# A hybrid mLSTM and GLA layer step: 60 loads and small transfers move from SyncE's DMA queue to GpSimd's

## The chip, the cores and the metric

The kernel runs on one core of one Trainium2 chip. The metric is the device time of the program in microseconds (us).

## The reference

One layer, fp32, for 256 prompt positions of one sequence and one further position of 8 decode sequences: T = 264 columns in all, D = 2048.

```
p = x @ w_in                                # 13 column groups: mLSTM q/k, v, i, f, o, z; GLA q, k, v, gate, z; two merge gates
q, k = silu(causal conv of width 4 (qk))    # 4 heads of 256
h, C', n', m' = mlstm(q, k, v, i, f, C, n, m)     # decode: C' = dec * C + w k v^T;  h from q . C'
ya = headnorm(h) * sigmoid(o) * silu(z) @ w_pa
o, S' = gla(gq, gk, gv, log gate, S)              # decode: S' = exp(gate) * S + k v^T;  o = q . S'
yb = headnorm_rms(o) * silu(bz) @ w_pb
y = (sigmoid(g_a) * ya + sigmoid(g_b) * yb) @ w_out
out = layernorm(alpha * x + y) * ln_g + ln_b      # returned with all new states
```

What matters here are the decode states: C is 8 x 4 x 256 x 256 and S is 8 x 4 x 128 x 256, 8 MB and 4 MB, each read, updated and written once.

## The kernel before

**Weights.** All products with a weight are TensorE products with the weight block as the stationary side and 264 columns moving. The weights come as 262 pieces of 128 x (8 x 128) fp32, 512 KB each. `load_raw` (L181) loads a piece on SyncE into one of 4 buffers (raw); `cast_piece` splits it: ACT rounds it (hi, L203), DVE subtracts (lo, L204). For each of a piece's 8 row blocks there are three matmuls: hi by x's high part (L223), hi by its low part (L224), lo by the high part (L227).

**Side work.** Between the weight products, generators do the rest in small steps; `pump` takes some steps after each unit. Each step is recorded with a priority, and a scheduler puts the instructions of ACT, DVE, GpSimd and SyncE in an order of its own; TensorE's order is that of the program text. An engine, and a DMA queue, takes its instructions in that order: one that waits holds up those behind it. 20 slots of 4 KB per partition (`t4`) are shared by raw results, spread rows and state chunks; a load waits until its slot's former content has been used, or stored.

**The two decode generators.** `g_a_decode` first puts k and q rows into a small DRAM tile (kq_d, L512), reads n (L507), and works through C in 16 chunks of 512 KB: `load` (cch, L526), ACT scales (L555), DVE adds k v^T (L571) and takes the product with q (L573), and GpSimd stores (sC, L564). The k and q rows come from kq_d, spread over all 128 partitions by `spread_rows` (kb, qb, L489), 512 KB each, 8 times. `g_gla_rows` writes exp(gate), k and q rows to rows_d (L674). `g_gla_decode` works through S in 8 chunks: `load` (sch, L778), and for every second chunk three spread tiles ga, gk, gq (L489); for each half chunk ACT forms gkv (L805), DVE multiplies (L807), adds (L808), multiplies by gq (L809) and reduces (L810). GpSimd stores the chunk (sS, L813).

`g_b_norm` follows: ACT squares (L822), DVE adds the two halves into ns (L824), once for each of four heads, TensorE sums over partitions with a matrix of constants (L829), and ACT and DVE do the rest (L831 to L838). In `g_a_prompt` GpSimd stores pC (L476); in `g_gla_prompt` TensorE does L707 on gq and gk. `g_ln_rows` loads the rows of the final norm (lgf L947, lbb L952).

Before the change SyncE issues all loads, and the stores to the DRAM tiles; GpSimd issues the stores of states.

Of the kernel before, what the change touches and what calls it, by code (L numbers as in the profile page):

```python
# [83 lines left out]
def body(ctx, tc, xT, wbig, wsmall, par, cmask, lmask, sel, rowc, gate, wgu, cT, sT, nst, cst, lnr,  # L84
         y, yd, pC, pn, pm, pconv, pS, sC, sn, sm, sS):
    nc = tc.nc
    V, A, G, PE = nc.vector, nc.scalar, nc.gpsimd, nc.tensor
# [12 lines left out]
    def t4(shape, name, dt=F32):  # L100
        return b4.tile(shape, dt, tag="b4", name=name)
# [21 lines left out]
    def side_ps():  # L123
        return ps_s.tile([128, 512], F32, tag="sd", name="sd")
# [19 lines left out]
    def P(name, j=0, n=None):  # L144
        o, w = PAR[name]
        return par_sb[:, o + j:o + (w if n is None else j + n)]
# [6 lines left out]
    def f(ap):  # L153
        return ap.bitcast(F32)
# [331 lines left out]
    def spread_rows(dst, src):  # L486

        n = src.shape[0] * src.shape[1]
        nc.sync.dma_start(out=dst.rearrange("p b d -> p (b d)"),  # L489
                          in_=src.rearrange("r d -> (r d)").unsqueeze(0).to_broadcast([128, n]))  # L490

    def g_a_decode():
        qT, kT, dw, decb = st["qT"], st["kT"], st["dw"], st["decb"]
        num, dmx, avd = st["num"], st["dmx"], st["avd"]
        qkd = one.tile([128, 2, H, NB, 2], F32, tag="qkd", name="qkd")
        for x, src in enumerate((qT, kT)):
            for q in range(2):
                V.tensor_copy(out=qkd[:, x, 2 * q:2 * q + 2].rearrange("p h b t -> p h t b"),
                              in_=src.slot(q)[:, :, L:T].rearrange("p (h t) b -> p h t b", t=2))
        yield 0.5  # L500
        qr = tmp.tile([64, 128], F32, tag="t1", name="qr", bufs=T1_BUFS)
        kr = tmp.tile([64, 128], F32, tag="t1", name="kr", bufs=T1_BUFS)
        nr = tmp.tile([64, 128], F32, tag="t1", name="nr", bufs=T1_BUFS)
        pt = side_ps()
        for x in range(2):
            PE.transpose(out=pt[0:64, x * 128:x * 128 + 128], in_=qkd[:, x].rearrange("p h b t -> p (h b t)"), identity=ident)
        nc.sync.dma_start(out=nr, in_=nst)  # L507
        A.copy(out=qr, in_=pt[0:64, 0:128])
        V.tensor_scalar(out=kr, in0=pt[0:64, 128:256], scalar1=dw[:, 1:2], scalar2=None, op0=ALU.mult)
        kq_d = dram.tile([2, 64, 128], F32, name="kq_d")  # L510
        for x, src in enumerate((kr, qr)):
            nc.sync.dma_start(out=kq_d[x], in_=src)  # L512
        yield 0.5
        dn = one.tile([64, 1], F32, tag="dn", name="dn")
        dx = one.tile([64, H * NB], F32, tag="dx", name="dx")
        scr = tmp.tile([64, 128], F32, tag="t1", name="scr8", bufs=T1_BUFS)
        V.scalar_tensor_tensor(out=nr, in0=nr, scalar=dw[:, 0:1], in1=kr, op0=ALU.mult, op1=ALU.add)
        V.scalar_tensor_tensor(out=scr, in0=nr, scalar=1.0, in1=qr, op0=ALU.mult, op1=ALU.mult, accum_out=dn)
        V.tensor_scalar(out=dx, in0=rc_sb[:, NB:NB + H * NB], scalar1=dn, scalar2=None, op0=ALU.mult)
        G.dma_start(out=sn, in_=nr)  # L520
        chunks = {}

        def load(i):
            if i < 16:
                c = t4([128, 4, 256], "cch")
                nc.sync.dma_start(out=c, in_=cT[i])  # L526
                chunks[i] = c

        load(0)
        yield 0.6  # L530
        pb = side_ps()[:, 0:H * NB]
        PE.matmul(pb, lhsT=ones[0:64, :], rhs=dx, start=True, stop=True)
        pb = pb.rearrange("p (h b) -> p h b", b=NB)
        ad = tmp.tile([128, H, NB], F32, tag="t1", name="add", bufs=T1_BUFS)
        A.activation(out=ad, in_=pb, func=AF.Abs)
        V.tensor_tensor(out=dmx[:, :, L:T], in0=dmx[:, :, L:T], in1=ad, op=ALU.max)
        yield 0.4
        scr2 = tmp.tile([128, 256], F32, tag="t1", name="scr", bufs=T1_BUFS)
        steps = [(h, b0, e) for h in range(H) for b0 in (0, 4) for e in range(2)]
        rows = {}  # L540

        def spread(i):

            if i < 16:
                h, b0, _ = steps[i]
                rows[h, b0] = t4([128, 4, 256], "kb"), t4([128, 4, 256], "qb")
                for x in range(2):
                    spread_rows(rows[h, b0][x], kq_d[x, 16 * h + 2 * b0:16 * h + 2 * b0 + 8, :])

        def scale(i):  # L550
            h, b0, e = steps[i]
            load(i + 1)
            c = chunks[i]
            for b in range(4):
                A.activation(out=c[:, b, :], in_=c[:, b, :], func=AF.Copy, scale=decb[:, h, b0 + b:b0 + b + 1])  # L555

        spread(0)
        scale(0)
        yield 1.6
        for i, (h, b0, e) in enumerate(steps):  # L560
            if e == 0:
                spread(i + 2)
            if i:
                G.dma_start(out=sC[i - 1], in_=chunks.pop(i - 1))  # L564
            if i + 1 < 16:
                scale(i + 1)
            kb, qb = rows[h, b0]
            c = chunks[i]
            nd = num.t(2 * h + e)
            for b in range(4):  # L570
                V.scalar_tensor_tensor(out=c[:, b, :], in0=kb[:, b, :], scalar=avd[:, 2 * h + e, b0 + b:b0 + b + 1],  # L571
                                       in1=c[:, b, :], op0=ALU.mult, op1=ALU.add)
                V.scalar_tensor_tensor(out=scr2, in0=c[:, b, :], scalar=1.0, in1=qb[:, b, :], op0=ALU.mult,  # L573
                                       op1=ALU.mult, accum_out=nd[:, L + b0 + b:L + b0 + b + 1])
                if b % 2:
                    yield 2.1
        G.dma_start(out=sC[15], in_=chunks.pop(15))
        st["ad_done"] = True
# [83 lines left out]
    def g_gla_rows():  # L662
        gq, gk, la = st["gq"], st["gk"], st["la"]
        gd = one.tile([128, 3, H, NB], F32, tag="gd", name="gd")
        A.activation(out=gd[:, 0], in_=la[:, :, L:T], func=AF.Exp, scale=TAU_INV)
        V.tensor_copy(out=gd[:, 1], in_=gk[:, :, L:T])
        V.tensor_copy(out=gd[:, 2], in_=gq[:, :, L:T])
        yield 0.4
        pt = side_ps()
        PE.transpose(out=pt[0:96, 0:128], in_=gd.rearrange("p x h b -> p (x h b)"), identity=ident)  # L670
        rows = tmp.tile([96, 128], F32, tag="t1", name="rows", bufs=T1_BUFS)
        A.copy(out=rows, in_=pt[0:96, 0:128])
        rows_d = dram.tile([96, 128], F32, name="rows_d")
        nc.sync.dma_start(out=rows_d, in_=rows)  # L674
        st["rows"] = rows_d
        yield 0.3

# [93 lines left out]
    def g_gla_decode():  # L771
        rows, oT, bvd = st["rows"], st["oT"], st["bvd"]
        chunks = {}

        def load(i):
            if i < 8:
                c = t4([128, 4, 2, 128], "sch")
                nc.sync.dma_start(out=c, in_=sT[i])  # L778
                chunks[i] = c

        load(0)
        yield 0.1
        spread = {}

        def rows_of(h):
            if h < H:
                spread[h] = [t4([128, NB, 128], "g" + x) for x in "akq"]
                for i, x in enumerate(spread[h]):
                    spread_rows(x, rows[32 * i + 8 * h:32 * i + 8 * h + 8, :])
# [3 lines left out]
        for h in range(H):  # L793
            rows_of(h + 1)
            ab, kb, qb = spread.pop(h)
            for bh in range(2):
                load(2 * h + bh + 1)
                c = chunks.pop(2 * h + bh)
# [141 lines left out]
    def g_ln_rows():  # L940


        ln["G"], ln["B"] = [], []
        for hf in range(2):
            gf, hi = t4([128, 1024], "lgf"), t4([128, 1024], "lgh", F32R)
            gg = t4([128, 1024], "lgg", F32R)
            nc.sync.dma_start(out=gf, in_=lnr[:, hf * 1024:hf * 1024 + 1024])  # L947
            A.copy(out=hi, in_=gf)
            V.scalar_tensor_tensor(out=gg, in0=f(hi), scalar=P("lnm"), in1=gf, op0=ALU.mult, op1=ALU.add)
            ln["G"].append(gg)  # L950
            bb = t4([128, 1024], "lbb")
            nc.sync.dma_start(out=bb, in_=lnr[64:65, hf * 1024:hf * 1024 + 1024].to_broadcast([128, 1024]))  # L952
            ln["B"].append(bb)
            yield 2.0

# [131 lines left out]
    def drain():  # L1087
# [5 lines left out]
    waiting += [  # L1093
        (("gates_done", "avt_done"), g_a_prompt),
        (("gates_done", "avt_done"), g_a_decode),
        (("gq_done", "gk_done", "gates_done"), g_gla_rows),
        (("gq_done", "gk_done", "bvt_done", "rows", "ap_done"), g_gla_prompt),
# [213 lines left out]
```

## Time and profile before

| | |
|---|---|
| median of 3 runs | 845.92 us (845.65 to 849.77) |
| the profiled execution | 848.47 us, span 846.7 us |
| its granted TensorE clock, mean | 0.993 of full speed |
| DMA | 184.76 MB, mean 218 GB/s |

The profile is of one execution, taken by the hardware. Its span runs from the first to the last recorded instruction; 1.8 us of the execution's time lie around it. PE is TensorE, DVE VectorE, ACT ScalarE, POOL GpSimd, and SPq is SyncE's queue of DMA issues. L223 is line 223 of the kernel. An engine's idle time in front of an instruction is put down to what came last of all that it waited for.

### The profile page before, as it was taken

To read this page: it belongs to the slowest core of one execution; us is meant where nothing else is said; L and a number is where in the kernel's file an instruction comes from. 1 tells how busy PE (TensorE), PEld (TensorE's weight loads), DVE (VectorE), ACT (ScalarE), POOL (GpSimd) and SP (SyncE) were. 2 spreads that over 40 slices of the span, in tenths; PEclk is the share of its full clock that TensorE was granted. 3 is DMA by queue.
4 is the path that set the end of the run, shared out by engine and by line. 5 is a ranking of instruction groups with operands and counts; after the bars stand their busy time and mean duration, and the time that the engine had idled before them with its cause. 6 is when DMAs were issued, how large, how long until landed. Compare 5 with 4: busy or idle time off the path is not lost.

```text
span 846.7 us, 16717 instructions
## 1 busy us (share of the span) xinstructions
PE 826.7 (98%) x6773; PEld 813.3 (96%) x6773; DVE 591.4 (70%) x964; ACT 451.4 (53%) x706; POOL 45.1 (5%) x75
## 2 busy tenths in 40 slices
PE   6999999999999999999999998999999999999996
PEld 6999999999899999999999998999999999999995
DVE  6877668545658788757579979994445766666962
ACT  5655457545445653555467747764444444444633
POOL 0000000000001000001000000310000000000410
PEclk9999999999999999999999998999999999999998
DMA  8765565558586985678687799756555555576513
GB/s 318 246 203 181 159 188 171 165 163 262 214 284 225 381 292 189 198 262 312 203 300 243 231 335 329 240 171 203 184 178 184 185 177 177 185 248 214 176 49 103
DMA packets 54766, 184.76 MB, mean 218 GB/s; under 512 B 8209, under 2 KB 9153, under 8 KB 54689
## 3 DMA queue, kind: packets, MB, share of 16 engines
q1 hardware_dynamic: 50560, 169.28, 61.3%
q0 software_dynamic: 4128, 14.42, 4.3%
q8 instruction: 53, 0.87, 0.4%
q14 instruction: 25, 0.20, 0.1%
HBM read 166.98 MB, written 16.69 MB: 217 GB/s over the span
## 4 chain that ended last, share of the span: by engine, by line
PE 81%; DMA 7%; DVE 6%; ACT 2%; issue 2%; SPq 1%; ACTq 0%; POOLq 0%; POOL 0%; DVEq 0%
PE mm L223 25%; PE mm L224 25%; PE mm L227 24%; DMA raw<-wbig 4%; DMA cch<-cT 4%; DVE lo L204 2%; ACT hi L203 1%; DVE scr L573 1%; PE sd L707 1%; PE sd L464 1%; DVE cch L571 1%; ACT cch L555 1%; PE sd L754 0%; SPq L489 0%; PE sd L420 0%
## 5 line engine op out<-in xcount | busy, mean ns | idle before, releaser
L223 PE MATMUL mm<-xh,hi 128*128 128x264 f32 x1552 | 447.2, 289 | 10.2 <-ACT hi L203 9.8
L224 PE MATMUL mm<-xl,hi 128*128 128x264 f32 x1552 | 441.2, 285 | 0.0
L227 PE MATMUL mm<-xh,lo 128*128 128x264 f32 x1536 | 437.2, 285 | 0.5 <-DVE lo L204 0.5
L203 ACT CAST hi<-raw 128x1024 fp32r<-128x1024 f32 (+1 forms) x260 | 267.9, 1034 | 279.5 <-PE mm L224 245.1
L204 DVE TENSOR_TENSOR lo<-raw,hi 128x1024 fp32r<-128x1024 f32 (+1 forms) x260 | 314.9, 1214 | 144.2 <-ACT hi L203 142.0
L223 PEld LDWEIGHTS mm<-xh,hi 128*128 128x128 f32 x1552 | 294.0, 189 | 12.5 <-ACT hi L203 10.0
L224 PEld LDWEIGHTS mm<-xl,hi 128*128 128x128 f32 x1552 | 294.2, 190 | 0.3
L227 PEld LDWEIGHTS mm<-xh,lo 128*128 128x128 f32 x1536 | 290.1, 189 | 1.0 <-DVE lo L204 1.0
L223 PE MATMUL mm<-mh,hi 128*128 128x264 f32 x256 | 72.9, 285 | 0.0
L224 PE MATMUL mm<-ml,hi 128*128 128x264 f32 x256 | 72.7, 284 | 0.0
L227 PE MATMUL mm<-mh,lo 128*128 128x264 f32 x256 | 72.4, 283 | 0.0
L555 ACT ACTIVATE cch<-cch,decb 128x256 f32<-128x256 f32 x64 | 28.0, 500 | 38.6 <-DMA cch<-cT 38.6
L571 DVE SCALAR_TENSOR_TENSOR cch<-kb,avd,cch 128x256 f32<-128x256 f32 x64 | 29.0, 479 | 27.8 <-ACT cch L555 27.8
L227 PEld LDWEIGHTS mm<-mh,lo 128*128 128x128 f32 x256 | 48.2, 188 | 0.0
L223 PEld LDWEIGHTS mm<-mh,hi 128*128 128x128 f32 x256 | 48.1, 188 | 0.0
L224 PEld LDWEIGHTS mm<-ml,hi 128*128 128x128 f32 x256 | 48.1, 188 | 0.0
L224 PE MATMUL mm<-ybl,hi 128*128 128x264 f32 x128 | 36.4, 284 | 0.0
L227 PE MATMUL mm<-yah,lo 128*128 128x264 f32 x128 | 36.4, 284 | 0.0
L223 PE MATMUL mm<-ybh,hi 128*128 128x264 f32 x128 | 36.4, 284 | 0.0
L224 PE MATMUL mm<-yal,hi 128*128 128x264 f32 x128 | 36.2, 283 | 0.0
L227 PE MATMUL mm<-ybh,lo 128*128 128x264 f32 x128 | 36.2, 283 | 0.0
L223 PE MATMUL mm<-yah,hi 128*128 128x264 f32 x128 | 36.2, 282 | 0.0
(323 smaller groups left out, 820.1 us busy)
## 6 DMA issues: line engine op xcount, KB each, us to landing
raw<-wbig SPq DMA_DIRECT2D x252, 512.0 KB, 4.7
cch<-cT SPq DMA_DIRECT2D x16, 512.0 KB, 8.6
sC<-cch POOLq DMA_DIRECT2D x16, 512.0 KB, 5.8
kb<-kq_d SPq DMA_DIRECT2D x8, 512.0 KB, 7.2
qb<-kq_d SPq DMA_DIRECT2D x8, 512.0 KB, 8.8
sch<-sT SPq DMA_DIRECT2D x8, 512.0 KB, 7.6
sS<-sch POOLq DMA_DIRECT2D x8, 512.0 KB, 6.7
xr<-xT SPq DMA_DIRECT2D x4, 528.0 KB, 7.1
```

The source lines that it names most:

```text
L203: A.copy(out=h, in_=r)
L204: V.tensor_tensor(out=lo, in0=r, in1=f(h), op=ALU.subtract)
L223: PE.matmul(out, lhsT=wh, rhs=rh, start=(k == k0), stop=False)
L224: PE.matmul(out, lhsT=wh, rhs=rl, start=False, stop=small and k == k1 - 1)
L227: PE.matmul(out, lhsT=los[n, k], rhs=rh, start=False, stop=(k == k1 - 1))
L464: PE.matmul(CN[:, 0:VC], lhsT=kw[:, s, d * 128:d * 128 + 128], rhs=vt[h // 2][:, s, h % 2, :], start=(s == 0), stop=(s == 1))
L555: A.activation(out=c[:, b, :], in_=c[:, b, :], func=AF.Copy, scale=decb[:, h, b0 + b:b0 + b + 1])
L571: V.scalar_tensor_tensor(out=c[:, b, :], in0=kb[:, b, :], scalar=avd[:, 2 * h + e, b0 + b:b0 + b + 1], in1=c[:, b, :], op0=ALU.mult, op1=A ...
L573: V.scalar_tensor_tensor(out=scr2, in0=c[:, b, :], scalar=1.0, in1=qb[:, b, :], op0=ALU.mult, op1=ALU.mult, accum_out=nd[:, L + b0 + b:L + ...
L707: PE.matmul(pl[s0:s0 + m, 4 * hf + h, n0:n0 + w].rearrange("p (n s) -> p n s", s=hs), lhsT=K[:, h, hf * 128 + s0:hf * 128 + s0 + m], rhs=r ...
```

## The change

Nine DMA statements are issued by GpSimd instead of SyncE, in all 60 DMAs: 28 spread tiles (kb, qb, ga, gk, gq), 16 chunks of C, 8 of S, the n rows, two stores to kq_d and one to rows_d, two loads each of lgf and lbb. SyncE keeps the weights, x, the constants and the stores of y.

```diff
     def spread_rows(dst, src):
...
-        nc.sync.dma_start(out=dst.rearrange("p b d -> p (b d)"),
-                          in_=src.rearrange("r d -> (r d)").unsqueeze(0).to_broadcast([128, n]))
+        G.dma_start(out=dst.rearrange("p b d -> p (b d)"),
+                    in_=src.rearrange("r d -> (r d)").unsqueeze(0).to_broadcast([128, n]))
...
     def g_a_decode():
...
-        nc.sync.dma_start(out=nr, in_=nst)
+        G.dma_start(out=nr, in_=nst)
...
-            nc.sync.dma_start(out=kq_d[x], in_=src)
+            G.dma_start(out=kq_d[x], in_=src)
...
-                nc.sync.dma_start(out=c, in_=cT[i])
+                G.dma_start(out=c, in_=cT[i])
...
     def g_gla_rows():
...
-        nc.sync.dma_start(out=rows_d, in_=rows)
+        G.dma_start(out=rows_d, in_=rows)
...
     def g_gla_decode():
...
-                nc.sync.dma_start(out=c, in_=sT[i])
+                G.dma_start(out=c, in_=sT[i])
...
     def g_ln_rows():
...
-            nc.sync.dma_start(out=gf, in_=lnr[:, hf * 1024:hf * 1024 + 1024])
+            G.dma_start(out=gf, in_=lnr[:, hf * 1024:hf * 1024 + 1024])
...
-            nc.sync.dma_start(out=bb, in_=lnr[64:65, hf * 1024:hf * 1024 + 1024].to_broadcast([128, 1024]))
+            G.dma_start(out=bb, in_=lnr[64:65, hf * 1024:hf * 1024 + 1024].to_broadcast([128, 1024]))
```

The order of the instructions follows from this. SyncE's queue before, in the middle of the GLA decode (xN is a number of equal ones in a row; 128x1024 is the tile):

```order
L778 DMA sch<-sT 128x1024
L181 DMA raw<-wbig 128x1024 x4
L489 DMA ga<-rows_d 128x1024
L489 DMA gk<-rows_d 128x1024
L489 DMA gq<-rows_d 128x1024
L778 DMA sch<-sT 128x1024 x2
L181 DMA raw<-wbig 128x1024 x2
L489 DMA ga<-rows_d 128x1024
L489 DMA gk<-rows_d 128x1024
L489 DMA gq<-rows_d 128x1024
L778 DMA sch<-sT 128x1024
L181 DMA raw<-wbig 128x1024 x4
```

In the changed kernel SyncE's queue holds only the raw rows of these. GpSimd's order there, changed:

```order
L778 DMA sch<-sT 128x1024 x2
L813 DMA sS<-sch 128x1024
L489 DMA ga<-rows_d 128x1024
L489 DMA gk<-rows_d 128x1024
L489 DMA gq<-rows_d 128x1024
L778 DMA sch<-sT 128x1024
L813 DMA sS<-sch 128x1024
L778 DMA sch<-sT 128x1024
L813 DMA sS<-sch 128x1024
L778 DMA sch<-sT 128x1024
L813 DMA sS<-sch 128x1024 x3
```

The loads now stand between the stores: the last three sch loads each have one sS store ahead of them.

VectorE's order at the end of the GLA decode and the start of `g_b_norm`, before:

```order
L204 TENSOR_TENSOR lo<-raw,hi 128x1024
L808 TENSOR_TENSOR sch<-sch,gkv 128x512
L809 TENSOR_TENSOR gpr<-sch,gq 128x512
L810 TENSOR_REDUCE oT_4886<-gpr 128x2x2
L204 TENSOR_TENSOR lo<-raw,hi 128x1024
L824 TENSOR_TENSOR ns<-nsq 128x264 x4
L204 TENSOR_TENSOR lo<-raw,hi 128x1024 x3
```

and changed:

```order
L808 TENSOR_TENSOR sch<-sch,gkv 128x512
L809 TENSOR_TENSOR gpr<-sch,gq 128x512
L204 TENSOR_TENSOR lo<-raw,hi 128x1024
L824 TENSOR_TENSOR ns<-nsq 128x264 x3
L810 TENSOR_REDUCE oT_4886<-gpr 128x2x2
L204 TENSOR_TENSOR lo<-raw,hi 128x1024
L824 TENSOR_TENSOR ns<-nsq 128x264
L204 TENSOR_TENSOR lo<-raw,hi 128x1024 x2
```

The last reduction and one lo moved behind the third ns, ahead of the fourth. TensorE's order is the same in both.

## Rows read from the trace of the kernel before

**Rows 1.** The first part of the page: busy time of each engine, its share of the span and its number of instructions.

```profile
PE 826.7 (98%) x6773; PEld 813.3 (96%) x6773; DVE 591.4 (70%) x964; ACT 451.4 (53%) x706; POOL 45.1 (5%) x75
```

**Rows 2.** What TensorE waited for: operation and line, what ended the wait; us in total, times, the longest.

```profile
PE mm L223 <- ACT hi L203: 9.8, 2, 7.2
PE sd L707 <- DVE gq L714: 1.5, 1, 1.5
PE sd L438 <- DVE E L430: 0.6, 1, 0.6
```

**Rows 3.** Windows, in us from the span's start: their length, the busy us of PE, PE's weight load, DVE, ACT and POOL (instructions), then the granted clock, the DMA share and GB/s.

```profile
480.00:500.00 20.00, 20.00 (x168) 20.00 (x167) 17.89 (x25) 10.95 (x24) 1.07 (x2) 1.00 0.88 314
500.00:520.00 20.00, 16.95 (x116) 16.43 (x115) 14.73 (x21) 10.86 (x24) 1.07 (x2) 0.83 0.95 327
300.00:320.00 20.00, 18.50 (x198) 18.04 (x196) 17.61 (x38) 10.77 (x15) 1.07 (x2) 1.00 0.85 285
491.17:541.15 49.98, 46.93 (x364) 46.41 (x363) 42.49 (x57) 31.95 (x65) 4.16 (x7) 0.93 0.88 306
487.00:489.00 2.00, 2.00 (x19) 2.00 (x19) 2.00 (x4) 1.98 (x5) 0.00 (x0) 1.00 1.03 414
600.00:620.00 20.00, 20.00 (x168) 20.00 (x168) 8.57 (x7) 7.87 (x11) 0.00 (x0) 1.00 0.56 182
```

**Rows 4.** TensorE's timeline at three places: start, busy us, engine, line, operation, tiles, shapes, how many in a row; in brackets the idle time before it and what ended that.

```profile
317.72 1.15 PE L707 MATMUL sd<-gq,gk 128*64 128x64 f32 x32 [1.50 <-DVE gq L714]
...
507.12 0.28 PE L227 MATMUL mm<-xh,lo 128*128 128x264 f32 x1
510.01 0.59 PE L223 MATMUL mm<-xh,hi 128*128 128x264 f32 x1 [2.60 <-ACT hi L203]
...
511.27 0.59 PE L227 MATMUL mm<-xh,lo 128*128 128x264 f32 x1 [0.45 <-DVE lo L204]
...
542.57 1.94 PE L829 MATMUL sd<-ns,inv 128*128 128x264 f32 x8
```

**Rows 5.** SyncE's queue in the timeline, 480 to 505: start and us of the issue (waits between issues are not in it).

```profile
483.85 2.23 SPq L181 DMA_DIRECT2D raw<-wbig  x2
490.76 0.33 SPq L489 DMA_DIRECT2D ga<-rows_d  x1
497.53 0.33 SPq L489 DMA_DIRECT2D gk<-rows_d  x1
...
499.47 0.38 SPq L778 DMA_DIRECT2D sch<-sT  x1
499.90 3.25 SPq L181 DMA_DIRECT2D raw<-wbig  x4
```

**Rows 6.** What SyncE's queue waited for in 480 to 515: us in total, times, the longest.

```profile
SPq L489 <- DMA sS<-sch: 11.0, 2, 6.4
```

**Rows 7.** The timelines of ACT (one cast) and of DVE.

```profile
508.91 1.04 ACT L203 CAST hi<-raw 128x1024 fp32r<-128x1024 f32 x1 [6.11 <-DMA raw<-wbig]
...
491.17 0.68 DVE L810 TENSOR_REDUCE oT<-gpr 128x4 f32<-128x512 f32 x1
...
496.33 1.23 DVE L204 TENSOR_TENSOR lo<-raw,hi 128x1024 fp32r<-128x1024 f32 x1 [1.79 <-ACT hi L203]
...
498.21 1.23 DVE L204 TENSOR_TENSOR lo<-raw,hi 128x1024 fp32r<-128x1024 f32 x1
499.35 0.68 DVE L810 TENSOR_REDUCE oT<-gpr 128x4 f32<-128x512 f32 x1
499.95 0.68 DVE L808 TENSOR_TENSOR sch<-sch,gkv 128x512 f32<-128x512 f32 x1
...
506.76 0.69 DVE L807 TENSOR_TENSOR sch<-sch,ga 128x512 f32<-128x512 f32 x1 [3.61 <-DMA sch<-sT]
...
509.99 1.23 DVE L204 TENSOR_TENSOR lo<-raw,hi 128x1024 fp32r<-128x1024 f32 x1 [0.73 <-ACT hi L203]
...
541.15 1.45 DVE L824 TENSOR_TENSOR ns<-nsq 128x264 f32<-128x264 f32 x4
```

**Rows 8.** DMA queues in 487 to 489: packets, MB, the time of their packets as a share of 16 engines' window. q1 is what SyncE issued, q0 what GpSimd issued.

```profile
q1 hardware_dynamic: 117, 0.43, 53.0%
q0 software_dynamic: 102, 0.40, 49.7%
```

**Rows 9.** DMA issues in 529 to 536: KB of each, us to landing.

```profile
sS<-sch POOLq DMA_DIRECT2D x1, 512.0 KB, 5.0
```

**Rows 10.** The view of the tile sch: time from issue to landing of the DMAs on it, in us.

```profile
DMA to landing us min/median/max: 4.2/7.1/11.8
```

**Rows 11.** The timelines of GpSimd, SyncE's queue and ACT, ahead of the wait at 317.72.

```profile
290.96 0.53 POOL L564 DMA_DIRECT2D sC<-cch  x1 [5.37 <-DVE cch L571]
...
300.18 0.65 SPq L526 DMA_DIRECT2D cch<-cT  x1
...
310.11 1.71 ACT L555 ACTIVATE cch<-cch,decb 128x256 f32<-128x256 f32 x4 [5.54 <-DMA cch<-cT]
```

**Rows 12.** The timelines of SyncE's queue and of GpSimd, 190 to 200.

```profile
195.30 0.38 SPq L489 DMA_DIRECT2D qb<-kq_d  x1
...
197.81 0.61 POOL L476 DMA_DIRECT2D pC<-pc  x1 [7.10 <-DVE pc L466]
```

**Rows 13.** The operations on the tile qb: ns min/median/max, first and last start in us.

```profile
L573 DVE SCALAR_TENSOR_TENSOR scr<-cch,qb x64: 360/417/427, 220.0 to 403.8; 128x256 f32<-128x256 f32 x64
```

## The prediction

> **What bounds the kernel now.** Read the engines' shares first: TensorE is busy 98% of the span, VectorE 70%, GpSimd 5% [rows 1]. A bound engine can only give back its idle time, so the next view is what PE waits for: 7.2 us at the start for the first weights (no moved DMA is ahead of them), then 2.6 at 510, 1.5 at 318 and 0.6 near 230 [rows 2, 4]. The windows say what the 510 wait costs in all: PE did 116 matmuls in 500 to 520 where the 20 us before held 168, at a granted clock of 0.83 against 1.00 [rows 3]. 52 missing of 168 in 20 us is 52/168 × 20 = **6.2 us**. Of these 2.6 + 0.45 are two waits; the rest is clock: after the 2.6 us gap a matmul takes 0.59 us for 0.28 [rows 4], the lower of the two levels (1.2 for 2.4 GHz). The 1.5 us gap at 318 was not followed by this: its window has a granted clock of 1.00 [rows 3]. So the saving has a bound: 6.2 + 1.5 + 0.6 = 8.3 us, 1.0% of the time.
>
> Next, why 510 came late, against the order of time. The weight cast (ACT L203) waited 6.11 us for its raw block [rows 7]. SyncE issued no weights from 486.1 to 499.90: ahead of them stand loads of the spread rows (L489), for whose buffers a store of sS had to land, 11.0 us in two waits, and one sch load [rows 5, 6]. DVE stood in the same queue's shadow: in 491.17 to 541.15 it was busy 42.49 of 49.98 us, idle 7.5, of which 1.79 waiting for a cast, 3.61 for sch (issued 499.47, there at 506.7) and 0.73 for a cast [rows 3, 5, 7]. That DVE has so little slack here decides the forecast.
>
> **The change part by part.** 60 DMAs leave SyncE's order and enter GpSimd's; matmuls and their order stay.
>
> *The 510 wait.* The L489 waits move to GpSimd, behind which no weight is queued. Weights then wait for their buffers alone, which were free at 486. I count the whole 6.2 us as gone: −6.2.
>
> *What is late next.* PE reaches b_norm's L829 at 542.57 now, without a wait; 6.2 earlier is 536.4. It needs the four ns of DVE L824, now begun at 541.15 [rows 4, 7]. What DVE does before that is unchanged by the change: 42.49 us from 491.17. By the changed order one L810 and one lo (0.68, 1.22) slip between the third and the fourth ns. The fourth is then done at 491.17 + 42.49 + 1.45 + 1.22 = 536.3, plus some 0.5 of small gaps (I leave standing a third of the 1.4 us of idle that the three waits above don't explain) = 536.8. PE wants the fourth three pairs of matmuls after the first: 8 of them took 1.94 [rows 4], so 6 take 1.45 and the need is at 537.8. DVE may lose 1.0 us on the way; every further one is a wait of PE.
>
> Does it lose more? sch chunk 5 is the place. GpSimd issues sS (third store), ga, gk, gq, sch, in this order. The third gk waits for the landing of that store, 497 as now, [rows 5], so sch goes out at about 498 to 498.6 (0.5 each), against 499.47. Until it lands, gk, gq and sch move 1.5 MB beside the weights. At 487 to 489 all DMA moved 414 GB/s at a share of 1.03 [rows 3], as much as any of these windows; weights alone need 182 (600 to 620); 232 are left, so 1.5 MB take 6.7 us from 497.5, and 504.2 is the earliest, 506.7 (as now) the latest: I add 1.1 to 1.6 for two queues that shared evenly (0.43 and 0.40 MB in the two us at 487 [rows 8]) and take **505.8**. DVE gets there after 10 state operations at 0.60 and three lo at 1.14 (start to start [rows 7]), 491.17 + 6.0 + 3.4 = 500.6. It idles 5.2 us, between 3.6 and 6.1. PE then waits 5.2 − 1.0 = **+4.2** at L829 (2.6 to 5.1).
>
> This wait falls into two: the first ns is done 2.5 us after PE wants it (533.8 without idle, + 5.2, − 536.4), the rest comes before the fourth. A gap of 2.6 lowered the clock, one of 1.5 did not [rows 2, 4], and 2.5 lies by the former; but the waits behind it may add. If it falls, 6.2 − 2.6 − 0.45 = 3.1 us of half speed come on top, as at 510. I count the two as even.
>
> The Trainium skill, "DMA: Bandwidth & Descriptors", section "Latency and other measured facts", gives about 1 us to the first byte on GpSimd's path and 0.6 on SyncE's. By it sch would land 0.4 later and the wait be 4.6. No row here separates the two, and the sum goes without it.
>
> *The 1.5 at 318 and the 0.6 at 230.* A cch chunk was issued at 300.18, behind weights that waited for buffers; ACT began on it at 310.11 after a wait of 5.54 us, and PE's L707 waited 1.50 behind DVE [rows 4, 11]. In GpSimd's queue the load stands behind the store issued at 290.96 and goes out by 292, 8 us earlier [rows 11]. Both waits are of side work that came late; neither can cost more than all of it: −1.5 and −0.6 (bound: nothing).
>
> *Edits costed at nothing.* GpSimd takes about 0.53 us for an issue [rows 11], 60 × 0.53 = 32 us of an engine that is busy 45 of 847. At its first place the new order delays: qb and the second cch stand behind the store pC, which waited for DVE until 197.81, so they go out some 3 us later than 195.30 [rows 12]. DVE first reads qb at 220.0 [rows 13]: over 10 us of cover even behind the longest landing below. Were it gone, DVE would be up to 3 us later there, and its lo with it. For lgf, lbb, nr, kq_d and rows_d none of PE's waits stands now [rows 2]; their issue order barely changes.
>
> **Sum**: −6.2 + 4.2 − 1.5 − 0.6 = −4.1 with the clock held, −1.0 with it lowered; the middle is −2.6. The profiled execution took 848.47 (span 846.7), 2.55 more than the median of the three runs, 845.92; its waits should be in all of them. 845.92 − 2.6 = **843.3**, the case's own range 840.5 to 846.
>
> **Rivals.**
> *All of it is gained.* If sch 5 lands by 501.6, DVE loses under 1.0 and PE never waits at L829: −8.3, 837.6; a store beside weights alone landed in 5.0 us [rows 9], which from 498.0 is 503.0, idle 2.4, wait 1.4 without loss of clock: −6.9, 839.0. For it: with the stall gone, weights are not drawn in a burst. Against it: the two spread loads ahead of it, and DMA shares of 0.88 and 0.95 on both sides of 500 [rows 3].
>
> *No change.* The 16 engines, not the queue, make the weights late: the bytes stay, and GpSimd's loads now compete with the weights instead of standing ahead of them. Then the 6.2 stays or moves to another block: 845.9 ± 1. For it: the share of 1.03 at 487 [rows 3]. Against it: for 14 us no weights were even issued [rows 5], and the share over 500 to 520 is below 1. The Trainium skill says in "DMA: Bandwidth & Descriptors", "Issuing engines are not separate DMA queues", that issuing from several engines saves only the time of issue, the transfers sharing the same engines. By this rule alone there would be no gain; the trace shows a wait ahead of the issue, in order, which the rule does not count.
>
> *Slower.* GpSimd's queue is in order too: the state loads now stand behind stores, and these behind DVE. Place: sch 5 to 7. Price: if each takes the longest of the sch rows, 11.8 us [rows 10], sch 5 is there at 509.8, DVE idles 9.2; a chunk is 8 operations at 0.60 and about four lo at 1.22, 9.8 us, so the next two add 2.0 each: 13.2. PE's wait is 12.2, the clock falls (+3.1): −8.3 + 12.2 + 3.1 = +7.0, 852.9. It decides from a DVE idle of 6.2 us (sum zero: 5.2 + 3.1 = 8.3); slower by over 0.5% from 10.4. For it: DVE without slack. Against it: 11.8 is the longest of all on this tile (median 7.1 [rows 10]).
>
> **How the numbers follow.** 0.5% (4.2 us) is about what a measurement of this kernel can tell from none. The forecast (gain mostly given back at L829) 0.53; all gained 0.22; no change 0.10; slower 0.15. Faster by over 0.5%, below 841.7: all of the second, and 0.10 of the forecast, where sch comes early and the clock holds: 0.32. Slower, above 850.1: nearly all of the last, 0.14. Same: 0.54. The range leaves out the far end of the last (0.12) and a little below 837.5: 837.5 to 850.0.
>
> **What would show it.** Right: no gap in weight issues at 486 to 500, no L223 wait near 510, no L707 wait; a DVE wait for sch of 4 to 6 us near 501 to 506; a PE wait at L829 of 3 to 5 us, with DVE ns as its releaser. Wrong: no wait at L829 (second case), an L223 wait on ACT behind raw remaining (third), DVE waits for sch of over 10 us or ACT waits for kb, qb or cch that reach PE (fourth).

## The result

| | before | changed |
|---|---|---|
| median | 846.02 us (845.65 to 849.77, 4 runs) | 859.14 us (855.93 to 860.73, 4 runs) |
| ratio | | 1.014, 95% interval 1.0099 to 1.0181 |
| profiled execution | 848.47 us, span 846.7 | 859.19 us, span 857.4 |

The kernel became slower by 13.1 us by the medians, 1.4% by the ratio of means; the forecast was 843.3, the range ended at 850.0. It lies on the side of the fourth case, and beyond that case's price of 852.9. The two profiled executions are 10.7 us apart; the profiled one of before was itself 2.45 above its median.

The profile after, read in the order of the prediction. The first part of the page (as [rows 1]) and what TensorE waited for (as [rows 2]; us in total, times, the longest):

```profile
PE 827.7 (97%) x6773; PEld 814.0 (95%) x6773; DVE 593.7 (69%) x964; ACT 451.7 (53%) x706; POOL 73.2 (9%) x135
```

```profile
PE mm L223 <- ACT hi L203: 7.6, 1, 7.6
PE mm L227 <- DVE lo L204: 5.4, 1, 5.4
PE sd L829 <- DVE ns L824: 4.0, 2, 3.5
PE sd L707 <- DVE gq L714: 1.5, 1, 1.5
```

The wait of 2.6 us for hi near 510 is gone, and so is the 0.6 at L438; the 1.5 at L707 is not. Two waits are new: 5.4 for lo and 4.0 at L829, both on DVE. Where they stand in TensorE's timeline (start, busy us, in brackets the idle time before), and the windows that answer to [rows 3] (length; busy us of PE, PE's weight load, DVE, ACT, POOL; granted clock, DMA share, GB/s):

```profile
515.17 0.59 PE L227 MATMUL mm<-xh,lo 128*128 128x264 f32 x1 [5.42 <-DVE lo L204]
...
547.38 2.19 PE L829 MATMUL sd<-ns,inv 128*128 128x264 f32 x6 [3.50 <-DVE ns L824]
550.05 1.25 PE L829 MATMUL sd<-ns,inv 128*128 128x264 f32 x2 [0.48 <-DVE ns L824]
```

```profile
480.00:500.00 20.00, 20.00 (x168) 20.00 (x167) 15.95 (x22) 11.27 (x25) 4.20 (x8) 1.00 0.89 321
500.00:520.00 20.00, 14.58 (x103) 14.38 (x102) 13.23 (x19) 11.47 (x25) 3.04 (x6) 0.85 0.76 262
540.00:560.00 20.00, 16.02 (x112) 14.69 (x112) 19.32 (x22) 12.37 (x20) 1.99 (x3) 0.91 0.69 235
492.00:498.00 6.00, 6.00 (x52) 6.00 (x52) 2.02 (x4) 2.52 (x4) 0.00 (x0) 1.00 1.02 414
```

500 to 520 now holds 103 matmuls where before it held 116 [rows 3]: at a full pace of 168 the stage loses 65/168 × 20 = 7.7 us, not 6.2. In 540 to 560 another 56 are missing, 6.7 us, 4.0 of it the wait at L829, the rest mostly the lowered clock (0.91). Before, that window held 161:

```profile
540.00:560.00 20.00, 20.00 (x161) 19.74 (x160) 20.00 (x21) 15.40 (x21) 6.48 (x6) 1.00 0.60 191
```

Why lo was late is read on DVE, between 491 and 515:

```profile
491.83 0.68 DVE L810 TENSOR_REDUCE oT<-gpr 128x4 f32<-128x512 f32 x1
496.49 1.29 DVE L807 TENSOR_TENSOR sch<-sch,ga 128x512 f32<-128x512 f32 x2 [3.98 <-DMA sch<-sT]
...
503.58 1.22 DVE L204 TENSOR_TENSOR lo<-raw,hi 128x1024 fp32r<-128x1024 f32 x1
504.71 0.68 DVE L809 TENSOR_TENSOR gpr<-sch,gq 128x512 f32<-128x512 f32 x1
512.09 0.69 DVE L807 TENSOR_TENSOR sch<-sch,ga 128x512 f32<-128x512 f32 x1 [6.70 <-DMA sch<-sT]
...
513.90 1.22 DVE L204 TENSOR_TENSOR lo<-raw,hi 128x1024 fp32r<-128x1024 f32 x1
```

It stood 3.98 and 6.70 us in front of operations on state chunks: on sch 3 and on sch 5 (the chunks are counted from 0, as in the prediction). The lo of 513.90 is behind the second of these in DVE's order; TensorE's wait ends with it. And why the chunks were late, on GpSimd (start, us of the issue, in brackets the idle time before):

```profile
482.02 0.54 POOL L813 DMA_DIRECT2D sS<-sch  x1 [7.70 <-DVE sch L808]
482.55 0.53 POOL L489 DMA_DIRECT2D gk<-rows_d  x1
483.07 0.53 POOL L489 DMA_DIRECT2D gq<-rows_d  x1
483.58 0.53 POOL L778 DMA_DIRECT2D sch<-sT  x1
484.36 0.53 POOL L778 DMA_DIRECT2D sch<-sT  x1 [0.24 <-DVE gpr L809]
490.35 0.54 POOL L813 DMA_DIRECT2D sS<-sch  x1 [5.46 <-DVE sch L808]
490.88 0.53 POOL L489 DMA_DIRECT2D ga<-rows_d  x1
498.08 0.53 POOL L489 DMA_DIRECT2D gk<-rows_d  x1 [6.68 <-DVE sch L807]
501.68 0.53 POOL L489 DMA_DIRECT2D gq<-rows_d  x1 [3.07 <-DMA sS<-sch]
502.20 0.53 POOL L778 DMA_DIRECT2D sch<-sT  x1
```

Four loads, 2 MB, were issued ahead of the store of 490.35 (gk, gq and sch 3 and 4, from 482.55 to 484.36). They landed one after the other, at 490.9, 493.8, 496.4 and 498.9, and the store behind them at 501.4, 11.1 us after its issue; before the change the third store, issued at 489.68, took 7.8. That is the longest landing of all DMAs on sS:

```profile
DMA to landing us min/median/max: 4.3/4.7/11.1
```

The landing released gq. Only then could gq and sch 5 be issued: 502.20, where before it was 499.47 [rows 5]. (The gk ahead of them had waited until 498.08 for the DVE operation that was itself late by the 3.98.) From its issue to its landing sch 5 took 9.9 us where before it took 7.2, so it was there at 512.1 instead of 506.7 [rows 7]. The pace of the queue is a row of the DMA queues in 492 to 498 (packets, MB, share of 16 engines):

```profile
q1 hardware_dynamic: 339, 1.25, 51.8%
q0 software_dynamic: 340, 1.24, 50.6%
```

Both queues had work, and each got half of the 414 GB/s: 0.21 MB in a us, 2.5 us for a load or store of 512 KB. That is about the spacing of the four landings above. The other half went to the weights, which SyncE now issued without the gap of before (a run of equal issues is one row, from the start of the first to the end of the last):

```profile
480.55 37.38 SPq L181 DMA_DIRECT2D raw<-wbig  x10
```

The last part of the loss is at the end. GpSimd's last long instruction is a DRAIN (count; ns min/median/max; first and last start; on its queue). Before, and after:

```profile
L1307 POOLq DRAIN  x3: 40/93/3394, 841.6 to 846.4; - x3
```

```profile
L1307 POOLq DRAIN  x3: 40/102/8289, 848.3 to 857.2; - x3
```

3.39 us became 8.29. SyncE's last issue was at 842.03 before; in the changed kernel it is 6.79 us later:

```profile
842.03 0.33 SPq L1052 DMA_DIRECT2D yd<-zd  x1
```

```profile
848.82 0.33 SPq L1052 DMA_DIRECT2D yd<-zd  x1
```

The span grew by 10.7, so 6.8 us were lost in the body and 3.9 behind the last issue. The DRAIN grew by 4.9, so some 1.0 us of the growth did not reach the end: before the change SyncE's own wait for the last stores covered the DRAIN by about that much.

### The profile page after: what moved, and what is told of

Read it like the earlier page. It is cut to its first block, busy times and chain, and to the rows that moved or that the text cites. A ratio compares the mean times of both kernels' runs of the same rounds, so it can differ in the third digit from the quotient of the medians.

```text
span 857.4 us, 16726 instructions
## 1 busy us (share of the span) xinstructions
PE 827.7 (97%) x6773; PEld 814.0 (95%) x6773; DVE 593.7 (69%) x964; ACT 451.7 (53%) x706; POOL 73.2 (9%) x135
## 4 chain that ended last, share of the span: by engine, by line
PE 38%; issue 11%; DMA 3%; DVE 1%; POOL 1%; ACT 0%; POOLq 0%; ACTq 0%; DVEq 0%
PE mm L223 12%; PE mm L227 12%; PE mm L224 12%; DMA sch<-sT 1%; DMA sS<-sch 1%; DMA sC<-cch 1%; DVE lo L204 0%; PE sd L829 0%; PE sd L996 0%; DVE oT L810 0%; PE sd L964 0%; DVE sch L807 0%; PE sd L1002 0%; PE zT L996 0%; DVE sch L808 0%
## 6 DMA issues: line engine op xcount, KB each, us to landing
cch<-cT POOLq DMA_DIRECT2D x16, 512.0 KB, 10.6
```

## The experiments

All ratios are to the kernel before, run beside it on the same chip, with 95% intervals (its medians there: 847.06 for e1 to e4, 847.37 for e6 to c3, 846.44 for c5 to e9, 846.84 for c8 to c12). The ratio is one of means, and the us behind it are worked out from it; where two runs are set side by side, their medians are. Waits are those of the one profiled execution of a run.

**e1_mlstm_only**: the change without its GLA part.

```diff
-        G.dma_start(out=rows_d, in_=rows)
+        nc.sync.dma_start(out=rows_d, in_=rows)
...
-                G.dma_start(out=c, in_=sT[i])
+                nc.sync.dma_start(out=c, in_=sT[i])
...
-                    spread_rows(x, rows[32 * i + 8 * h:32 * i + 8 * h + 8, :])
+                    spread_rows(x, rows[32 * i + 8 * h:32 * i + 8 * h + 8, :], nc.sync)
```

> Only the mLSTM part of the change (n rows, kq_d, cch, kb, qb) and lgf, lbb, 39 DMAs, go through GpSimd's queue; the GLA part (rows_d, ga, gk, gq, sch) stays with SyncE. Theory: the loss of the change has two parts. One is GpSimd's last instruction of the program, a DRAIN that took 3.39 us with 35 DMAs issued by GpSimd and 8.29 with 95, 0.082 us per DMA; before, it ended 1.0 us ahead of SyncE. The other is the GLA decode: state loads, spread rows and state stores in one queue. So here: DRAIN 0.53 + 74 x 0.082 = 6.6 us, 2.2 us on the end; TensorE about as before, with the wait near 510 and without the one of 0.6: 847.5 us. Rival (the mLSTM part delays the decode as a whole and so causes the late GLA chunk): TensorE loses about 7 as with the whole change, 855.

Measured: 848.00, ratio 1.0024 (1.0007 to 1.0040), +2.0 us. The DRAIN took 6.58 us. The mLSTM part costs its DRAIN and nothing that can be told. The wait near 510 that was expected to stay was 0.2 us in the profiled execution, though the GLA part is as before; 1.8 stood at L829 and 0.7 in front of lo.

**e2_gla_only**: the other half (rows_d, ga, gk, gq and sch stay on GpSimd, all else goes back).

> Only the GLA part of the change (rows_d, ga, gk, gq, sch), 21 DMAs, goes through GpSimd's queue. Theory (loss at the GLA decode from one queue for loads and stores, and a DRAIN by the number of DMAs): DRAIN 0.53 + 56 x 0.082 = 5.1 us, 0.7 on the end; the waits of VectorE for sch and of TensorE for lo and ns as with the whole change, 6 to 8 us: 853 to 854 us. Rival (the mLSTM part is the cause): the wait near 510 goes and nothing comes for it, 838 to 841.

Measured: 853.14, ratio 1.0083 (1.0052 to 1.0113), +7.0 us; DRAIN 5.11. TensorE's waits, as above:

```profile
PE mm L223 <- ACT hi L203: 7.5, 1, 7.5
PE sd L829 <- DVE ns L824: 4.4, 2, 4.2
PE mm L227 <- DVE lo L204: 2.4, 2, 1.3
```

The two new waits come with the GLA part alone. The rival (the mLSTM part delays everything) is out.

**e3_tiny60**: the kernel before and 60 DMAs of 4 bytes on GpSimd; the order of the other engines is that of before.

```diff
+            if kind == "pab" and j == 4:
+                scr60 = const.tile([128, 60], F32, name="scr60")
+                for z in range(60):
+                    G.dma_start(out=scr60[0:1, z:z + 1], in_=f(mh.t(3))[0:1, z:z + 1])
```

> The kernel before with 60 more DMAs on GpSimd's queue, each of one element of 4 bytes from SBUF to SBUF, issued while GpSimd is idle (after mh is written, past 590 us); no other engine's order changes. Theory (the DRAIN at the end costs 0.082 us for each DMA that GpSimd issued, whatever it moved): DRAIN 8.3 us, 3.9 us later end, 849.9 us. Rival (it goes by bytes or descriptors that went through this queue, 14.4 MB before and 43.9 after): DRAIN 3.4 to 3.5 us, 846.0 us.

Measured: 850.06, ratio 1.0054 (1.0034 to 1.0074), +4.6 us. GpSimd's DRAINs:

```profile
L1311 POOLq DRAIN  x3: 40/103/8294, 839.1 to 847.9; - x3
```

8.29 us, as with the 60 large ones. The run shows one thing more. The order of all other engines is that of before, and the 60 DMAs come past 590 us; yet in its profiled execution the wait near 510 is 1.2 us and not 2.6, and 1.5 stands at L829. Two of its windows, as [rows 3]:

```profile
500.00:520.00 20.00, 18.07 (x135) 17.64 (x134) 16.53 (x22) 11.18 (x24) 1.59 (x3) 0.91 0.96 334
520.00:540.00 20.00, 18.50 (x153) 18.28 (x152) 19.03 (x26) 16.12 (x32) 2.56 (x4) 1.00 0.77 271
```

33 and 15 matmuls are missing, 3.9 and 1.8 us, where the profiled execution of before lost 6.2 and nothing. What this stage loses, and where, differs from execution to execution of one order.

In all runs the longest DRAIN goes by the number of DMAs that GpSimd issued:

| DMAs on GpSimd | 35 | 47 | 51 | 56 | 74 | 86 | 87 | 95 | 95 (tiny) |
|---|---|---|---|---|---|---|---|---|---|
| DRAIN, us | 3.39 | 4.37 | 4.70 | 5.11 | 6.58 | 7.56 | 7.64 | 8.29 | 8.29 |

(8.29 − 3.39)/60 = 0.082 us each. In these runs bytes and shapes made no difference.

**e4_rows_only**: ga, gk and gq alone on GpSimd.

> Only ga, gk and gq, 12 DMAs, go through GpSimd's queue; sch stays with SyncE. Theory: DRAIN 0.53 + 47 x 0.082 = 4.4 us, hidden behind the last stores of y. The weights no longer stand behind the wait of the spread rows for the sS store; the sch loads share a queue with weights only, so the stores have two loads in their queue ahead of them instead of four: sS lands in 7 to 9 us, the fifth chunk by about 506. The wait near 510 goes, part comes back ahead of ns: 840 to 845, 842 us. Rival (any load that shares the stores' queue delays the chunk as the whole change did): 852 us.

Measured: 849.50, ratio 1.0036 (1.0015 to 1.0057), +3.0 us: a miss, 4.5 above the theory's range, and less than the rival's 852. No wait near 510, but 4.4 us at L829 and 1.9 for lo; DVE waited 6.9 us for sch. Four loads ahead of the stores are not needed for the loss; even the rows alone delay them (the store of 501.46, right behind gk and gq, landed after 10.9 us).

**e6_rows_once**: the change, with ga, gk, gq loaded for one head only.

```diff
+                if h:
+                    spread[h] = spread1[0]
+                    return
...
+                spread1.append(spread[h])
```

> The whole change, but ga, gk and gq are loaded for the first head alone and used for all four (the decode rows of the other heads are not loaded, so their results use the first head's): 9 loads of 512 KB fewer in GpSimd's queue, 86 DMAs in all. Theory (the fifth state chunk is late because loads and stores stand in one queue behind each other, and VectorE's lo instructions stand behind the operation that waits for it): VectorE waits for sch under 2 us in all, TensorE does not wait for lo, and under 3 us at L829. DRAIN 0.53 + 86 x 0.082 = 7.6 us, 3.2 on the end; body 4 to 8 us shorter than before: 841 to 847, 844 us. Rival (a load through GpSimd's queue is slow by itself): the waits stay, 855 to 860.

Measured: 844.75, ratio 0.9975 (0.9959 to 0.9990), although its DRAIN took 7.56 us. DVE waited for sch once, 2.5 us; TensorE waited 1.1 at L829 (L833 in this kernel) and not for lo. Nine loads of 512 KB fewer in GpSimd's queue end the loss, so a load through that queue is not slow by itself. This takes away bytes as well as places in the queue; it doesn't tell the two apart.

**e8_stores_apart**: the change, with the sS stores issued by ScalarE.

```diff
-                G.dma_start(out=sS[2 * h + bh], in_=c)
+                A.dma_start(out=sS[2 * h + bh], in_=c)
```

> The whole change, but the eight sS stores are issued by ScalarE on its own queue, so that they don't stand behind loads: 87 DMAs on GpSimd. Theory: the stores land within 8 us instead of 11, the third frees its slot by 498, the fifth sch chunk lands by 506; part of the loss at the decode goes: VectorE waits for sch 4 to 6 us in all instead of 12, TensorE waits 2 to 4 us at L829 and not for lo; DRAIN 7.6 us, 3.3 on the end: 846 to 850 us. Rival (the loads are late whatever the stores do): as the whole change, 856 to 860.

Measured: 855.29, ratio 1.0100 (1.0082 to 1.0118), +8.5 us, of which 3.3 by the DRAIN (worked out from its 7.64 us and the cover of 1.0): a miss, 5.3 above the theory's range, and just below the rival's. TensorE doesn't wait for lo, but 5.0 us at L829; DVE waits 6.7 for sch, 5.85 of it for sch 5:

```profile
507.24 0.69 DVE L807 TENSOR_TENSOR sch<-sch,ga 128x512 f32<-128x512 f32 x1 [5.85 <-DMA sch<-sT]
```

The third store landed in 6.2 us, by 495.5, and sch 5 was issued at 496.61, earlier than the prediction had it; it still took 10.6 us to land, with gk and gq (494.07, 496.09) ahead of it. So the store behind loads is one part of the cause, and the slow landing of the load itself is another. Both queues had work then; no run holds the weights back, so how much of that landing is the rows ahead and how much the weights' half isn't shown.

**c1_pool_mul** and **c3_rows_pool_mul**: the product L809 on GpSimd, with the DMAs of before, and with ga, gk, gq on GpSimd.

```diff
-                    V.tensor_tensor(out=pr, in0=cc, in1=qb[:, q].unsqueeze(2).to_broadcast(sh), op=ALU.mult)
+                    G.tensor_tensor(out=pr, in0=cc, in1=qb[:, q].unsqueeze(2).to_broadcast(sh), op=ALU.mult)
```

> The kernel before, with the GLA decode's product by gq (L809, 16 operations of 0.60 us) on GpSimd instead of VectorE; all DMAs as before. Theory (VectorE is the engine without slack between 440 and 540 us, and chunk stores, slots and loads follow its pace): VectorE has 9.7 us less to do there, the stores of sS go out earlier, the wait of the spread rows for them and with it TensorE's wait near 510 shrink: 840 to 844 us. Rival (the product on GpSimd lengthens the chain of a chunk, or slows VectorE by sharing its port, and the reduce waits for it): 848 or more.

> ga, gk and gq through GpSimd's queue (12 DMAs) and the product by gq (L809) on GpSimd. Theory (with the wait near 510 gone TensorE reaches L829 earlier and VectorE, with 9.7 us less work, is there too; the DRAIN of 4.4 us is hidden): neither wait, 6 to 8 us below the kernel before: 839 to 842 us. Rival (a load that waits in GpSimd's order now also holds up the products behind it, and with them VectorE's reduce): no better than the rows alone, 849 or more.

Measured: 850.98, ratio 1.0036 (1.0019 to 1.0054), and 858.16, ratio 1.0124 (1.0106 to 1.0141). In both the rival came true. The product took 2.14 us (median) on GpSimd for 0.69 on DVE, and DVE waited for it 14.2 us in all in the first. Relief for DVE that lengthens the chain of a chunk is none.

**c5_lo_pool** and **c6_lo_pool_rows_act**: the lo of 8 pieces on GpSimd, alone, and with ga, gk, gq issued by ScalarE.

```diff
-            V.tensor_tensor(out=lo, in0=r, in1=f(h), op=ALU.subtract)
+            (G if i in range(146, 168, 3) else V).tensor_tensor(out=lo, in0=r, in1=f(h), op=ALU.subtract)
```

> The kernel before with the lo subtraction of 8 weight pieces (every third of 146 to 167, those of the GLA decode) on GpSimd instead of VectorE; all DMAs as before. Theory (VectorE without slack between 440 and 540 sets the pace of chunks and their stores): 8 x 1.14 = 9 us less on VectorE there, the sS stores go out earlier, the wait near 510 shrinks: 841 to 845 us. Rival (a lo takes 4 us or more on GpSimd and is late for TensorE, or holds up the stores behind it): 848 or more.

> As the one with 8 lo on GpSimd, and ga, gk, gq issued by ScalarE on its own queue, so that weights don't stand behind them and no DMA is added to GpSimd. Theory: neither the wait near 510 nor one at L829: 838 to 842 us. Rival (ScalarE's casts now stand behind the spread rows' wait for the sS stores, as the weights did): a wait on hi or lo of several us, 846 to 852.

Measured: 849.27, ratio 1.0044 (1.0026 to 1.0061), and 855.89, ratio 1.0112 (1.0091 to 1.0133). Misses: in the first, in the range of its rival, the wait near 510 stayed (3.0) with 2.6 for lo; the second has 6.2 at L829 and 4.6 for lo, which is above the ranges of theory and rival.

**c7_cch_only**: only the 16 cch loads on GpSimd.

> Only the 16 cch loads go through GpSimd's queue. Theory: DRAIN 0.53 + 51 x 0.082 = 4.7 us, 0.3 on the end; of the waits at 318 and 230 (1.5 and 0.6) up to 2 us go; the GLA decode as before: 845 to 847 us, no difference that can be told. Rival (a state load behind stores in GpSimd's order is late there as in the GLA decode): 850 or more.

Measured: 845.77, ratio 0.9994 (0.9979 to 1.0008): no difference, as expected.

**e9_act_queue**: chunks and spread rows through ScalarE's queue.

> The whole change, but cch, sch and all spread rows (52 DMAs) are issued by ScalarE on its own queue; the eight others stay on GpSimd, 43 DMAs there. Theory (the cost of the change is GpSimd's DRAIN, and loads that share one queue and one order with the stores): DRAIN 4.0 us, hidden; stores land in 6 to 8 us; the fifth sch chunk is there by 505; some loss from casts that stand behind a waiting load: 842 to 849 us. Rival (any second queue of loads beside the weights makes the state chunks late, as with the stores apart): sch loads land in 10 us or more, waits for lo or ns of 5 us: 850 to 855.

Measured: 858.13, ratio 1.0148 (1.0125 to 1.0170). A miss, above the ranges of theory and rival: as slow as the change, with a DRAIN of only 4.05 us (43 DMAs), which adds nothing to the end. TensorE waited 9.1 us at L829, and 5.4 where a matmul waited for ScalarE's copies out of PSUM (gr, bzr). DVE waited 8.6 us for sch; sch 5 went out at 507.58 and landed 9.9 us later. So a state chunk is late behind waiting rows in another queue than GpSimd's too. But ScalarE's own work stood behind those waits as well (7.3 us for the landing of one sS store, ahead of gkv), and the run doesn't tell how much of the loss is that.

**c8_paced**, **c9_after_paced**, **c11_rows_paced**, **c12_gla_paced**: the GLA decode takes one step per unit of weights instead of two, so that L829 stands 14 pieces later in TensorE's order; with the DMAs of before, of the change, with ga, gk, gq moved, and with the GLA part moved.

```diff
-        for _ in range(BACK_STEPS):
+        for b in range(BACK_STEPS):
             for g in [g for g in side if g.__name__ in BACK][:1]:
-                if budget > 0:
+                if budget > 0 and (b == 0 or g.__name__ == "g_a_decode"):
```

> The kernel before, with the GLA decode written at one step per unit of weights instead of two, so that TensorE's L829 stands 336 matmul rows (14 weight pieces, about 40 us) later in its order; all DMAs on their queues of before. Theory (the wait near 510 is of the queue that weights share with waiting loads, L829 has nothing to do with it): the wait near 510 stays, none at L829: 844 to 848 us, no difference. Rival (the decode itself spreads out and neither wait is left): 838 to 841.

> The whole change, with L829 14 pieces later in TensorE's order in the same way. Theory (the late decode costs TensorE twice: where lo stands behind the wait for the fifth chunk on VectorE, and at L829 because it follows at once): the L829 wait of 4.0 us and its loss of clock go, the wait for lo and the 3.9 us of the DRAIN stay: 850 to 853 us against 859 with the change alone. Rival (the lateness moves to the next thing that needs the decode, yb): 857 or more.

> ga, gk and gq (12 DMAs) through GpSimd's queue, and L829 14 pieces later in TensorE's order. Theory: the wait near 510 goes, the L829 wait of the run with the rows alone (4.4 us) goes, about 2 us of wait for lo stays, the DRAIN of 4.4 us is hidden behind the stores of y: 841 to 844 us, faster than before. Rival (what was gained near 510 is given back at lo or at yb): 846 to 850.

> The GLA part of the change (21 DMAs) through GpSimd's queue, and L829 14 pieces later in TensorE's order. Theory: the L829 wait of the run with this part alone (4.4 us) goes, the 2.4 us of lo stay, DRAIN 5.1 us, 0.7 on the end: 841 to 845 us. Rival (a chunk that is late through this queue costs the same wherever L829 stands): 851 to 854.

Measured: 840.51, ratio 0.9916 (0.9902 to 0.9930); 853.90, ratio 1.0080 (1.0066 to 1.0093); 845.28, ratio 0.9974 (0.9959 to 0.9990); 847.30, ratio 1.0006 (0.9992 to 1.0020). The first beats both kernels, by its rival's way, not by mine. The second is 0.9 us above its theory's range; the third and fourth lie above their theories' ranges and below those of their rivals. The first's waits of TensorE, two of its windows, and SyncE's queue:

```profile
PE mm L223 <- ACT hi L203: 7.6, 1, 7.6
PE sd L707 <- DVE gq L714: 0.8, 1, 0.8
```

```profile
500.00:520.00 20.00, 20.00 (x168) 20.00 (x167) 14.94 (x20) 11.82 (x25) 1.06 (x2) 1.00 0.93 336
...
540.00:560.00 20.00, 20.00 (x168) 20.00 (x167) 18.46 (x22) 11.06 (x17) 2.56 (x4) 1.00 0.71 224
```

```profile
484.44 1.50 SPq L778 DMA_DIRECT2D sch<-sT  x1
488.03 15.06 SPq L181 DMA_DIRECT2D raw<-wbig  x6
503.19 0.70 SPq L778 DMA_DIRECT2D sch<-sT  x1
504.49 0.33 SPq L181 DMA_DIRECT2D raw<-wbig  x1
504.87 0.63 SPq L489 DMA_DIRECT2D ga<-rows_d  x1
505.63 0.86 SPq L181 DMA_DIRECT2D raw<-wbig  x1
506.54 0.60 SPq L489 DMA_DIRECT2D gk<-rows_d  x1
```

With the decode written later, six weights stand ahead of the rows in the one queue, where before two stood there and then a gap of nearly 14 us [rows 5]. Neither window is short, and no wait is left but those at the start and at L707. DVE still waits 12.1 us for sch in all, as in the changed kernel, but in four waits of at most 4.9, and no lo is late. The edit does two things at once, L829 later and the queue in another order; the run doesn't tell them apart.

In c9 the wait at L829 is gone, as the theory had it, and the waits for lo became five, 6.2 us in all. The clock stays full (1.00 from 500 to 560): 500 to 520 holds 153 matmuls, 520 to 540 holds 147, and 540 to 560 holds 144:

```profile
PE mm L223 <- ACT hi L203: 7.5, 1, 7.5
PE mm L227 <- DVE lo L204: 6.2, 5, 2.0
```

```profile
540.00:560.00 20.00, 17.61 (x144) 17.20 (x142) 16.33 (x20) 12.24 (x25) 2.56 (x4) 1.00 0.76 262
```

Two comparisons can be made, and they answer different questions. Against the change c9 is 5.2 us shorter (859.14 to 853.90; SyncE's last issue 848.82 to 842.72): that is what the late place of L829 gives back, about what the theory took off. Against c8 it is 13.4 longer, 3.9 of it by the DRAIN: that is what the queue costs where no wait near 510 is left to gain. The change is 13.1 above its own before, nearly the same number, but it is what is left after the change has also removed the stall near 510, so the two are not one cost. Likewise c11 is 4.2 us shorter than e4 and c12 5.8 shorter than e2, and they lie 4.8 and 6.8 above c8. So part of the loss is a matter of L829's place, some 4 to 6 us in these runs, and the rest, late lo and DRAIN, stays wherever it stands.

## Why the prediction was wrong

- **The 510 wait, −6.2: right in its mechanism, and the size of one execution.** SyncE issued weights throughout and hi was in time; no wait of TensorE for hi is left there. But "its waits should be in all of them" doesn't hold: e3, in the order of before, waited 1.2 there and 1.5 at L829.
- **sch 5 at 505.8: the step that failed.** It was issued at 502.2, not at 498 to 498.6, and was there at 512.1, 6.3 us late. Some 3.9 of this is the issue. I took the landing of the third store "497 as now". That store had been alone in GpSimd's queue; the change put four loads ahead of it, 2 MB at 0.21 MB/us, and it landed at 501.4. I counted the loads' new place and not what the new loads do to what was in that queue before. The other 2.4 is the landing: 9.9 us from the issue where the prediction had 7.2 to 7.8. e6 and e8 show both sides: with fewer loads DVE hardly waits for sch; with the stores apart the issue is early (496.61) and the landing still slow (10.6), and the time is still 8.5 above before.
- **DVE's idle 5.2: 3.98 + 6.70 = 10.7.** The 3.98 is a wait for sch 3, the third of the four loads in a row (issued 483.58, there at 496.4); the prediction had no wait for it. The prediction's fourth case began its loss at 6.2 and had 13.2; in size the truth lies between.
- **The price, +4.2 at L829: paid in two places.** I charged the idle of DVE to L829 alone. DVE takes its instructions in order, so the lo behind the waiting operation came late too, and TensorE waited 5.42 us for it, with a lowered clock behind it (0.85 in 500 to 520), before the wait of 4.0 at L829. That these 4.0 lie by the forecast's 4.2 is luck: they are what is left of a loss twice as large. (The share of it that the prediction gives to the first ns, 533.8 + 5.2 − 536.4, is 2.6 and not 2.5; nothing hangs on it.)
- **The end: a term that was not in the sum.** I costed the 60 issues at nothing, by GpSimd's idle time. Each also lengthens the DRAIN at the end by 0.082 us, and of 4.9 us only 1.0 was covered: +3.9. The trace of before showed the DRAIN of 3.39 us; no row there said what it depends on. e3 shows it.
- **−1.5 and −0.6.** The wait at L707 stayed at 1.5, the other one went. The cch loads did go out early, at 288 to 290, and ACT waited 2.7 us for one instead of 5.5, but DVE then waited 3.1 for a cast. In e3, in the order of before, the wait at L707 is 0.2, and in e1 and c7 it is 0.2 or gone, so it differs from run to run; it was no sure gain.
- **The slower case** named the right place, sch 5 in an in-order queue that loads and stores share, with a chance of 0.15. It had loads late behind stores; the trace shows a store late behind loads first. It lacked the wait for lo and the DRAIN, and its time, 852.9, fell short by 6.
- **The sum by what was measured**, from the profiled executions: 7.7 − 6.2 = +1.5 in 500 to 520, (161 − 112)/168 × 20 = +5.8 in 540 to 560, −0.6 at L438: 6.7 (7.2 with the 0.5 of 520 to 540, 164 matmuls for 168), against 6.8 at SyncE's last issue; with 3.9 at the end 10.7. The other 2.4 of the 13.1 are the profiled run of before, slower than its median by that: in e3, whose order is the same, the last issue is at 839.58 and not 842.03.

The Trainium skill, "DMA: Bandwidth & Descriptors", section "Queues, rings and completion order", says that a DMA engine goes round between the queues that have work, by packets. This case agrees: 51.8% and 50.6%. The rule of the same page of the Trainium skill that the prediction weighed (issuing from several engines saves only the issue) fits what was moved, 414 GB/s at 487 to 489 before and at 492 to 498 after, and leaves out the order: c8 gets 7 of the 8.3 us, the bound of the prediction, inside one queue.

## What to carry to other kernels

Moving loads to another queue moves them in front of whatever was in that queue; cost what stands there already, and follow the landing that each store owes to a buffer. An in-order engine that waits holds up everything behind it, so charge its idle time to the first instruction behind it that the bound engine wants, and not to the last alone. A wait in a shared queue may be cured by order: c8, where six weights stand ahead of the rows and L829 comes later, reached 0.9916 (0.9902 to 0.9930) with every DMA on its queue of before. Before a wait is counted as a gain, look whether other executions of the same order have it.

## What the runs showed of the hardware

- The DRAIN on GpSimd at the end of the program takes 0.53 us + 0.082 us for each DMA that GpSimd issued, 35 to 95 of them, whether of 4 bytes or 512 KB.
- A 128x512 product of two fp32 tiles took 2.14 us (median; 1.26 to 2.79) on GpSimd and 0.69 on VectorE; a 128x1024 subtraction 2.41 us (2.38 to 3.71) for 1.22.
